# A second seven-product block in every up-projection group, and one fewer in every down-projection half

## The chip, the cores and the metric

The kernel runs on one core of a Trainium2 chip. The metric is the device time of one execution in microseconds, as the median of several runs. A profiled execution gives a trace of the engines: TensorE (PE, with its weight loads as PEld), VectorE (DVE), ScalarE (ACT), GpSimd (POOL, which only issues transfers here) and SyncE (SP, which issues the weight loads from HBM).

## The reference, cut to what matters

The program is a two-layer encoder trunk on 256 rows of 2048 features. Each layer is a mixer (attention of several kinds) and then a gated feed-forward part; a final normalisation ends it. The change lies in the feed-forward parts, which are

```python
def conv_ffn(x, w_up, conv_w, conv_b, w_down):
    h = jnp.einsum("bsd,df->bsf", x, w_up)              # 2048 -> 2 * 5632
    g, u = h[..., :D_FF], h[..., D_FF:]
    gp = jnp.pad(g, ((0, 0), (1, 1), (0, 0)))
    g = conv_w[0] * gp[:, :-2] + conv_w[1] * gp[:, 1:-1] + conv_w[2] * gp[:, 2:] + conv_b
    return jnp.einsum("bsf,fd->bsd", jax.nn.gelu(g) * u, w_down)   # 5632 -> 2048
```

and before each of them `rmsnorm` of the rows. All data are float32.

## The kernel before, in words

**A product in three.** A float32 number is split into a high part (rounded by a cast on ACT, `split`, L231) and a low part (what the cast left, a subtraction on DVE, L234). A float32 product becomes three products on PE: high by high, high by low, low by high (L195 to L197). A weight *unit* is a tile of 128 by 1024, that is two blocks of 128 features by 512 columns; `wunit` loads it (`raw`, five buffers), splits it (`wh` and `wl`, four buffers each), and `a_products` issues 12 matmuls for it: two blocks, two halves of the rows, three products.

**Seven products for eight.** Two units of two neighbouring column chunks, with 256 features and 256 rows, form a 2 by 2 by 2 block product, which needs eight block products or, by the known scheme of Winograd, seven. `column_forms` makes the sums of the weights (four DVE subtractions of 128x512, L951 to L955) and splits them; `form_sums` makes the sums of the activations, with `split` after it; `seven_products` issues 21 matmuls (L977 to L979) where two units issue 24. Three of the seven results go straight into the accumulators (`gm`), four go into banks of their own (`extra`: tags `s` and `tp`) and are added on DVE later.

**The feed-forward part.** `ffn` runs two halves (`HALVES`: six and five groups). `up_group(layer, j)` makes 512 columns of the gate (side x = 0) and of the other branch (x = 1) from 16 units: u = 0 to 3 of both sides by turns, then the rest of side 0, then the rest of side 1. At u = 3 (`UPK`) both sides' units are one seven-product block; its extra results are summed by `extra_parts` (L844 to L848) and scaled by `scaled_parts` (L856). At the end of a side, DVE scales and adds the two accumulators into a tile (L878; `sc` for side 0, `z` for side 1) and transposes it in 32 by 32 pieces (`turned`, L279); 16 transfers then move the pieces into place (`moved`, L273: 12 issued by POOL, 4 by SP). When side 0 has landed, `convolved` does the convolution in the next group (ACT L896, then two DVE instructions for each of four feature tiles, L897 and L899, then GELU, L901). When side 1 has landed, `multiplied` multiplies (L928) and splits the result into the activations of the down projection (`prod`). For the groups j - g0 in the third entry of `HALVES`, it also makes the activation sums of a seven-product block (`row_forms`).

**The down projection.** After a half's groups, `chunk_pair` does column chunks 0 and 1, then 2 and 3: its head (`pair_head`) takes both chunks by turns and does the blocks in `seven` as seven products; the rest follows chunk by chunk.

**Order.** The code's `later` and `tick` say after which unit a deferred step is written. A scheduler then sets the order in which each engine's instructions stand. On the chip each engine takes its instructions in that order, and a waiting instruction holds up those behind it.

Of the kernel before, what the change touches and what calls it, by code (L numbers as in the profile page):

```python
# [27 lines left out]
F32 = mybir.dt.float32  # L28
F32R = mybir.dt.float32r
AF = mybir.ActivationFunctionType  # L30
# [3 lines left out]
P = 128  # L34
# [13 lines left out]
RAW = 5  # L48
AHEAD = 4
LAST = 2  # L50
UPK = 3
HALVES = ((0, 6, (1, 2, 3)), (6, 11, (1, 2, 3)))


def rev2(ap):
# [16 lines left out]
def trunk_kernel(ctx: ExitStack, tc, a, out):  # L72
    nc = tc.nc
    V, S, G, T = nc.vector, nc.scalar, nc.gpsimd, nc.tensor

    const = ctx.enter_context(tc.tile_pool(name="const", bufs=1))
    wts = ctx.enter_context(tc.tile_pool(name="wts", bufs=4))
    acts = ctx.enter_context(tc.tile_pool(name="acts", bufs=1))
    att = ctx.enter_context(tc.tile_pool(name="att", bufs=2))
    tmp = ctx.enter_context(tc.tile_pool(name="tmp", bufs=2))  # L80
# [5 lines left out]
    def nm(s):  # L86
        uid[0] += 1
        return f"{s}_{uid[0]}"
# [5 lines left out]
    def later(delay, fn, rank=2):  # L94

        pending.append((now[0] + delay, rank, fn))
# [19 lines left out]
    def tps(tag, bufs):  # L116
        return psum.tile([P, 512], F32, name=nm(tag), tag=tag, bufs=bufs)
# [187 lines left out]
    def turned_rows(c, gain, res):  # L305

        z = att.tile([P, 2, 512], F32, name=nm("z"), tag="sc", bufs=1)
        V.transpose(z, h[:, :, c * 512:(c + 1) * 512])
        pf = att.tile([P, 8, P], F32, name=nm("hT"), tag="pt", bufs=2)
        moved(z.rearrange("p t k -> p (t k)"), pf)  # L310

        def tiles():
            for j in range(4):
                res[c * 4 + j] = y_tile(pf.rearrange("p (t j) q -> p j t q", t=2)[:, j], gain, c * 4 + j)
            if res is formed.get("of") and c == UPK // 2:
                y_forms(pf.rearrange("p (t j) q -> p j t q", t=2), gain)
        return tiles

    formed = {}

    def form_sums(a11, a21, a12, a22):

        f = tmp.tile([P, 4, P], F32, name=nm("sums"), tag="scc")
        V.tensor_tensor(f[:, 0], a21, a22, op=ALU.add)
        V.tensor_tensor(f[:, 1], f[:, 0], a11, op=ALU.subtract)
        V.tensor_tensor(f[:, 2], a11, a21, op=ALU.subtract)
        V.tensor_tensor(f[:, 3], a12, f[:, 1], op=ALU.subtract)
        return f

    def y_forms(src, gain):  # L330

        y = tmp.tile([P, 2, 2, P], F32, name=nm("yf"), tag="ry")
        for k in range(2):
            S.activation(y[:, k], src[:, UPK % 2 * 2 + k], AF.Copy, scale=gain[:, 2 * UPK + k:2 * UPK + k + 1])
        f = form_sums(*(y[:, k, t] for k in range(2) for t in range(2)))
        form = []
        for x, tag in enumerate(("R", "Rq")):
            high = tmp.tile([P, 2, P], F32R, name=nm("form"), tag="t0")
            low = const.tile([P, 2, P], F32R, name=nm("form"), tag=tag, bufs=1)
            split(high, low, f[:, 2 * x:2 * x + 2])  # L340
            form += [(high[:, k], low[:, k]) for k in range(2)]
        formed["form"] = form

    def row_factor(pin=False, late=False):

# [209 lines left out]
    yT = []  # L555
# [276 lines left out]
    yT = mixer_out(a["ev_out"], mix, ln[:, 2, :])  # L832


    def up_group(layer, j, yT, rstd, prod, *more):

        sides, extra, sums = {}, [], []
        src = [a["up"][layer, j, x] for x in range(2)]

        def extra_parts():  # L840

            b1, b5, b6, b7 = extra
            s1, x0, x1, y1 = (tmp.tile([P, 512], F32, name=nm("sum"), tag=tag) for tag in ("rx", "ry", "ry", "rx"))
            S.copy(s1, b1)  # L844
            V.tensor_tensor(x0, s1, b6, op=ALU.add)  # L845
            V.tensor_tensor(x1, x0, b7, op=ALU.add)
            V.tensor_tensor(x0, x0, b5, op=ALU.add)
            V.tensor_tensor(y1, x1, b5, op=ALU.add)  # L848
            sums.extend([[s1, x1], [x0, y1]])
            later(1, scaled_parts)  # L850

        def scaled_parts():

            for x in range(2):
                for t in range(2):
                    S.activation(sums[x][t], sums[x][t], AF.Copy, scale=rstd[0][:, t:t + 1])  # L856

        pss = [[tps("gm", 4), tps("gm", 4)] for _ in range(2)]
        for u in range(4):
            if not j and u == 2:  # L860
                rstd.append(row_factor())
            if u == UPK:
                extra += [tps("s", 2), tps("tp", 2), tps("tp", 2), tps("s", 2)]
                seven_products(pss, extra, column_forms(src, u, True), u, yT, formed["form"], True, True)
                later(1, extra_parts)
            else:
                for x in range(2):
                    a_unit(pss[x], src[x], u, yT, KT)
            tick()
        for x in range(2):  # L870
            for u in range(4, 8):
                a_unit(pss[x], src[x], u, yT, KT)
                if u % 2 == 1:
                    tick()
            z = (tmp.tile([P, 8, P], F32, name=nm("z"), tag="z", bufs=1) if x else
                 new_sc().rearrange("p t (f k) -> p (t f) k", k=P))
            for t in range(2):
                out = V.scalar_tensor_tensor(z.rearrange("p (f t) k -> p t f k", t=2)[:, t],  # L878
                                       pss[x][t].rearrange("p (f k) -> p f k", k=P), rstd[0][:, t:t + 1],
                                       sums[x][t].rearrange("p (f k) -> p f k", k=P), op0=ALU.mult, op1=ALU.add)  # L880
                if t:
                    tc.keep_in_program_order(out)
            sides[x] = quad(2 * x)
            turned(z.rearrange("p b k -> p (b k)"), sides[x].rearrange("p f (t k) -> p (f t) k", k=P), (3,))
            if not x:
                later(2, lambda: convolved(layer, j, sides))
        later(2, lambda: multiplied(j, sides, prod, *more))
# [14 lines left out]

    def new_forms(g0, n):

        if n == 0:
            high = tmp.tile([P, 4, P], F32R, name=nm("form"), tag="rw", bufs=1)
            return [(high[:, 2 * x:2 * x + 2], att.tile([P, 2, P], F32R, name=nm("form"), tag="bias", bufs=2))
                    for x in range(2)]
        if g0:
            t = acts.tile([P, 2, 4, P], F32R, name=nm("form"), tag=f"act{18 + 2 * n}")  # L910
        else:
            t = att.tile([P, 2, 4, P], F32R, name=nm("form"), tag="pt", bufs=2)
        return [(t[:, 0], t[:, 1])]

    def row_forms(c4, parts):

        f = form_sums(*(c4[:, 2 + k, t * P:(t + 1) * P] for k in range(2) for t in range(2)))
        form = []
        for high, low in parts:
            n = high.shape[1]  # L920
            split(high, low, f[:, len(form):len(form) + n])
            form += [(high[:, x], low[:, x]) for x in range(n)]
        return form
# [42 lines left out]
    def seven_products(pss, extra, w, u, act, form, first, last):  # L966

        def block(k, t):
            return [act[2 * u + k][:, x, t * P:(t + 1) * P] for x in range(2)]

        s1, s2, s3, s4 = form
        b1, b5, b6, b7 = extra
        for ps, (ah, al), (wh, wl) in zip(
                (pss[0][0], pss[1][0], b1, b7, b5, b6, pss[0][1]),
                (block(1, 0), s4, block(0, 0), s3, s1, s2, block(1, 1)), w):
            own = any(ps is x for x in extra)
            T.matmul(ps, ah, wh, start=own and first, stop=False)  # L977
            T.matmul(ps, ah, wl, start=False, stop=False)  # L978
            T.matmul(ps, al, wh, start=False, stop=own and last)  # L979
# [51 lines left out]
    def ffn(layer, yT, gain, last=False):  # L1031
        rstd, res = [], None
        for g0, g1, seven in HALVES:
            prod, forms = [], {}
# [13 lines left out]
    yT = ffn(0, yT, ln[:, 1, :])  # L1048
# [109 lines left out]
    for hh in range(2):  # L1158
        vt = v_tiles(gemm_a(a["od_v"][hh], yT, KT), rstd, ((18, 19, 20, 21), (16, 17, 22, 23))[hh])
        for hd in range(hh * 4, hh * 4 + 4):  # L1160
            y = att.tile([P, 6, 64], F32, name=nm("nb"), tag="bias", bufs=2)
# [8 lines left out]
            q, k = qk_tiles([a["od_qk"][hd * 2 + x] for x in range(2)], yT, (Rq, R), (rev, None), hd % 2 * 2)  # L1170
            later(2, lambda hd=hd, q=q, k=k, vt=vt, y=y: d_head(hd, q, k, vt, y))
    yT = mixer_out(a["od_out"], mix, ln[:, 3, :])
# [156 lines left out]
def _paired_up(w):  # L1329

    w = w.copy()
    x, y = w[:, :, 0, UPK].copy(), w[:, :, 1, UPK].copy()
    w[:, :, 0, UPK] = np.concatenate([x[..., :512], y[..., :512]], axis=-1)
    w[:, :, 1, UPK] = np.concatenate([y[..., 512:], x[..., 512:]], axis=-1)
    return w


# [69 lines left out]
```

## Time and profile before

| what | value |
|---|---|
| median of 3 runs | 2412.46 us (2407.63 to 2412.59) |
| the profiled execution's own time | 2409.76 us |
| its span | 2407.9 us |
| PE busy, weight loads busy | 99%, 82% of the span |
| DVE, ACT, POOL busy | 77%, 57%, 22% |
| mean granted TensorE clock | 0.999 |
| DMA traffic | 505.64 MB, mean 210 GB/s |

The span is what the profile covers from the first to the last instruction; the execution's own time is 1.9 us more. A matmul's row shows its time through the array, so that matmuls that follow each other overlap in the trace; busy shares of PE therefore tell whether PE was ever empty, not how fast it went. Rows of the timeline give the start in us, the length, the engine, line and operation, the tiles (out<-in), how many instructions are merged, and in brackets how long the engine had been idle and what ended that.

### The profile page before, as it was taken

How to read it: one execution, taken by the hardware profiler on the slowest of the kernel's cores; microseconds unless marked ns; L12 is line 12 of the kernel's file. 1: busy time of each engine (PE TensorE's matmuls, PEld its weight loads, DVE VectorE, ACT ScalarE, POOL GpSimd, SP SyncE). 2: the span in 40 equal slices, each digit the busy share in tenths (PEclk: the TensorE clock that was granted, in tenths of full speed). 3: DMA queues.
4: the chain of work that ended last, by engine and by line, in shares of the span. 5: the costliest groups of instructions: out<-in, count | busy, mean ns of one | idle time of the engine just before them, and what ended most of it. 6: DMA issues, size and time to landing. Idle time of an engine off the chain costs nothing.

```text
span 2407.9 us, 32958 instructions
## 1 busy us (share of the span) xinstructions
PE 2387.8 (99%) x10895; PEld 1982.4 (82%) x10895; DVE 1860.2 (77%) x2461; ACT 1374.0 (57%) x1954; POOL 538.8 (22%) x940
## 2 busy tenths in 40 slices
PE   9999999999999999999999999999999999999998
PEld 7888888888888888888788888888888888888787
DVE  6576567666778888778889868676788887788887
ACT  7455455566656565445656657555565654456564
POOL 1132033322222422004232100422223320033220
PEclk9999999999999999999999999999999999999999
DMA  8778678766777877668777764667778876687874
GB/s 309 203 195 239 196 196 239 216 201 184 218 200 221 213 214 217 202 206 219 213 217 211 221 201 138 193 197 211 201 214 225 208 227 195 207 219 209 236 212 156
DMA packets 287531, 505.64 MB, mean 210 GB/s; under 512 B 159096, under 2 KB 160504, under 8 KB 287360
## 3 DMA queue, kind: packets, MB, share of 16 engines
q1 hardware_dynamic: 256848, 470.15, 65.0%
q0 software_dynamic: 30080, 32.74, 8.0%
q8 instruction: 85, 1.39, 0.2%
q14 instruction: 86, 0.70, 0.1%
q10 hardware_dynamic: 432, 0.66, 0.1%
HBM read 458.48 MB, written 2.18 MB: 191 GB/s over the span
## 4 chain that ended last, share of the span: by engine, by line
PE 45%; DVE 3%; DMA 1%; issue 1%; ACT 1%; SPq 0%; POOL 0%; DVEq 0%; ACTq 0%
PE gm L197 12%; PE gm L196 12%; PE gm L195 12%; PE gm L145 2%; PE gm L150 1%; DVE wl L234 1%; PE gm L978 1%; PE gm L979 1%; PE gm L977 1%; PE tp L978 1%; DVE form L234 1%; DMA qk<-z 1%; ACT wh L231 1%; PE tp L979 0%; PE s L979 0%
## 5 line engine op out<-in xcount | busy, mean ns | idle before, releaser
L231 ACT CAST wh<-raw 128x1024 fp32r<-128x1024 f32 (+1 forms) x897 | 935.7, 1048 | 820.7 <-PE gm L197 651.5
L234 DVE TENSOR_TENSOR wl<-raw,wh 128x1024 fp32r<-128x1024 f32 (+1 forms) x897 | 1085.1, 1216 | 391.3 <-ACT wh L231 384.1
L195 PE MATMUL gm<-wh,yT 128*128 128x512 f32 x2092 | 816.1, 390 | 0.0
L196 PE MATMUL gm<-wl,yT 128*128 128x512 f32 x2092 | 814.7, 389 | 0.3 <-DVE wl L234 0.3
L197 PE MATMUL gm<-wh,yT 128*128 128x512 f32 x2092 | 814.6, 389 | 0.0
L197 PEld LDWEIGHTS gm<-wh,yT 128*128 128x128 f32 x2092 | 392.6, 188 | 82.2 <-DVE yT L240 0.2
L196 PEld LDWEIGHTS gm<-wl,yT 128*128 128x128 f32 x2092 | 392.8, 188 | 81.8 <-DVE wl L234 1.4
L195 PEld LDWEIGHTS gm<-wh,yT 128*128 128x128 f32 x2092 | 392.8, 188 | 80.9 <-ACT junk L265 0.4
L273 POOL DMA_DIRECT2D qk<-sc x264 | 151.7, 583 | 863.9 <-issue 389.6
L273 POOL DMA_DIRECT2D qk<-z x392 | 225.6, 584 | 257.7 <-DVE z L279 227.2
L195 PE MATMUL gm<-wh,prod 128*128 128x512 f32 x518 | 201.5, 389 | 0.0
L197 PE MATMUL gm<-wh,prod 128*128 128x512 f32 x518 | 201.5, 389 | 0.0
L196 PE MATMUL gm<-wl,prod 128*128 128x512 f32 x518 | 201.5, 389 | 0.0
L195 PEld LDWEIGHTS gm<-wh,prod 128*128 128x128 f32 x518 | 97.2, 188 | 20.3
L196 PEld LDWEIGHTS gm<-wl,prod 128*128 128x128 f32 x518 | 97.2, 188 | 20.2
L197 PEld LDWEIGHTS gm<-wh,prod 128*128 128x128 f32 x518 | 97.2, 188 | 20.2
L196 PE MATMUL gm<-wl,mix 128*128 128x512 f32 x256 | 100.1, 391 | 0.9 <-DVE wl L234 0.9
L195 PE MATMUL gm<-wh,mix 128*128 128x512 f32 x256 | 100.0, 391 | 0.0
L197 PE MATMUL gm<-wh,mix 128*128 128x512 f32 x256 | 99.6, 390 | 0.0
L273 POOL DMA_DIRECT2D hT<-z x72 | 41.4, 583 | 199.8 <-PE gm L197 75.5
L856 ACT ACTIVATE sum<-sum,rstd 128x512 f32<-128x512 f32 x88 | 59.7, 718 | 17.7 <-DVE sum L845 10.0
L145 PE MATMUL gm<-yT,wh 128*128 128x512 f32 x256 | 59.5, 390 | 0.0
(356 smaller groups left out, 2644.1 us busy)
## 6 DMA issues: line engine op xcount, KB each, us to landing
raw<-in_up SPq DMA_DIRECT2D x352, 512.0 KB, 4.5
raw<-in_down SPq DMA_DIRECT2D x176, 512.0 KB, 4.4
raw<-in_eva_qk SPq DMA_DIRECT2D x96, 512.0 KB, 4.3
raw<-in_eva_v SPq DMA_DIRECT2D x46, 512.0 KB, 6.0
raw<-in_evb_qk SPq DMA_DIRECT2D x32, 512.0 KB, 4.7
raw<-in_ev_out SPq DMA_DIRECT2D x32, 512.0 KB, 4.3
raw<-in_od_qk SPq DMA_DIRECT2D x32, 512.0 KB, 4.3
raw<-in_od_out SPq DMA_DIRECT2D x32, 512.0 KB, 4.3
```

The lines of the kernel that those rows point to most:

```text
L145: T.matmul(ps.rearrange("p a b -> p (a b)"), wh[:, k * P:(k + 1) * P], act[u * 8 + k].rearrange("p a b -> p (a b)"), start=(u == 0 and k = ...
L150: T.matmul(ps[:, 1, :], wl[:, k * P:(k + 1) * P], act[u * 8 + k][:, 0, :], start=False, stop=(u * 8 + k == KT - 1))
L195: T.matmul(ps[t], ah, wh[:, sl], start=(kt == 0), stop=False)
L196: T.matmul(ps[t], ah, wl[:, sl], start=False, stop=False)
L197: T.matmul(ps[t], al, wh[:, sl], start=False, stop=(kt == nk - 1))
L231: first = S.copy(dst_h, src)
L234: V.tensor_tensor(dst_l, src, dst_h.bitcast(F32), op=ALU.subtract)
L273: (nc.sync if i in on_sync else G).dma_start(dst[j * 32:(j + 1) * 32, :, i * 32:(i + 1) * 32], z[i * 32:(i + 1) * 32].rearrange("p (b j c) ...
L856: S.activation(sums[x][t], sums[x][t], AF.Copy, scale=rstd[0][:, t:t + 1])
L977: T.matmul(ps, ah, wh, start=own and first, stop=False)
L978: T.matmul(ps, ah, wl, start=False, stop=False)
L979: T.matmul(ps, al, wh, start=False, stop=own and last)
```

## The change

Each up-projection group has seven-product blocks at u = 3 and u = 5 (`UPKS`), so that units 0 to 5 of both sides go by turns and only units 6 and 7 are done side by side; the four extra banks collect both blocks and are summed after the second. Each half of the down projection has two blocks (j - g0 = 1, 2) instead of three. The activation sums for u = 5 are made once per layer (`y_forms`) and live in the buffers `rw` and `bias`, which the third down block used.

```diff
-UPK = 3
-HALVES = ((0, 6, (1, 2, 3)), (6, 11, (1, 2, 3)))
+UPKS = (3, 5)
+HALVES = ((0, 6, (1, 2)), (6, 11, (1, 2)))
...
-            if res is formed.get("of") and c == UPK // 2:
-                y_forms(pf.rearrange("p (t j) q -> p j t q", t=2), gain)
+            for n, u in enumerate(UPKS):
+                if res is formed.get("of") and c == u // 2:
+                    y_forms(pf.rearrange("p (t j) q -> p j t q", t=2), gain, n, u)
...
         pss = [[tps("gm", 4), tps("gm", 4)] for _ in range(2)]
-        for u in range(4):
+        heads = UPKS[-1] + 1
+        for u in range(heads):
             if not j and u == 2:
                 rstd.append(row_factor())
-            if u == UPK:
-                extra += [tps("s", 2), tps("tp", 2), tps("tp", 2), tps("s", 2)]
-                seven_products(pss, extra, column_forms(src, u, True), u, yT, formed["form"], True, True)
-                later(1, extra_parts)
+            if u in UPKS:
+                if not extra:
+                    extra += [tps("s", 2), tps("tp", 2), tps("tp", 2), tps("s", 2)]
+                seven_products(pss, extra, column_forms(src, u, True), u, yT, formed[u], u == UPKS[0], u == UPKS[-1])
+                if u == UPKS[-1]:
+                    later(1, extra_parts)
             else:
                 for x in range(2):
                     a_unit(pss[x], src[x], u, yT, KT)
             tick()
         for x in range(2):
-            for u in range(4, 8):
+            for u in range(heads, 8):
                 a_unit(pss[x], src[x], u, yT, KT)
```

The host's layout of the weights follows (`_paired_up`). In the rows below, a name's number tells one tile from the next; a line behind L315 is 6 to 10 higher in the changed kernel than before.

Where the instructions stand now, first on DVE at the end of an up group (the fifth of the first half, layer 0). `wl` is the low part of one weight unit. Before, from the end of side 0 to the end of side 1:

```order
L878 SCALAR_TENSOR_TENSOR sc_7935<-gm_7667,rstd_6182,sum_7850 128x4x128
L878 SCALAR_TENSOR_TENSOR sc_7935<-gm_7668,rstd_6182,sum_7852 128x4x128
L279 STREAM_TRANSPOSE sc_7935<-sc_7935 128x1024
L234 TENSOR_TENSOR wl_8013<-raw_8010,wh_8012 128x1024
L234 TENSOR_TENSOR wl_8070<-raw_8067,wh_8069 128x1024
L234 TENSOR_TENSOR wl_8088<-raw_8085,wh_8087 128x1024
L234 TENSOR_TENSOR wl_8106<-raw_8103,wh_8105 128x1024
L878 SCALAR_TENSOR_TENSOR z_8042<-gm_7669,rstd_6182,sum_7851 128x4x128
L878 SCALAR_TENSOR_TENSOR z_8042<-gm_7670,rstd_6182,sum_7853 128x4x128
L279 STREAM_TRANSPOSE z_8042<-z_8042 128x1024
```

Now, the same place:

```order
L888 SCALAR_TENSOR_TENSOR sc_8024<-gm_7704,rstd_6197,sum_7975 128x4x128
L234 TENSOR_TENSOR wl_8066<-raw_8063,wh_8065 128x1024
L888 SCALAR_TENSOR_TENSOR sc_8024<-gm_7705,rstd_6197,sum_7977 128x4x128
L234 TENSOR_TENSOR wl_8109<-raw_8106,wh_8108 128x1024
L279 STREAM_TRANSPOSE sc_8024<-sc_8024 128x1024
L888 SCALAR_TENSOR_TENSOR z_8081<-gm_7706,rstd_6197,sum_7976 128x4x128
L234 TENSOR_TENSOR wl_8127<-raw_8124,wh_8126 128x1024
L888 SCALAR_TENSOR_TENSOR z_8081<-gm_7707,rstd_6197,sum_7978 128x4x128
L234 TENSOR_TENSOR wl_8159<-raw_8156,wh_8158 128x1024
L279 STREAM_TRANSPOSE z_8081<-z_8081 128x1024
```

The transpose of side 0 stood four unit splits ahead of the first instruction of side 1; it now stands directly ahead of it (`wl_8066` belongs to the group's last unit, `wl_8109` to the next group's first).

On DVE in the next group, from the convolution on, before (`t` and `form` are the weight difference and its low part; the five raw-to-`wl` rows are two units and the three splits of the block):

```order
L899 SCALAR_TENSOR_TENSOR qk_8028<-qk_7938,convw,qk_8028 128x255 x2
L234 TENSOR_TENSOR wl_8173<-raw_8170,wh_8172 128x1024
L952 TENSOR_TENSOR raw_8192<-raw_8193,raw_8192 128x512
L234 TENSOR_TENSOR wl_8200<-raw_8193,wh_8199 128x1024
L234 TENSOR_TENSOR form_8210<-t_1509_8196,form_8209 128x512
L954 TENSOR_TENSOR raw_8193<-raw_8193,t_1509_8196 128x512
L234 TENSOR_TENSOR wl_8206<-raw_8192,wh_8205 128x1024
L955 TENSOR_TENSOR raw_8193<-raw_8193 128x512
L928 TENSOR_TENSOR qk_8028<-qk_8028,qk_8045 128x1024
L234 TENSOR_TENSOR wl_8214<-raw_8193,wh_8213 128x1024
```

Now:

```order
L909 SCALAR_TENSOR_TENSOR qk_8142<-qk_8027,convw,qk_8142 128x255 x2
L234 TENSOR_TENSOR wl_8253<-raw_8246,wh_8252 128x1024
L234 TENSOR_TENSOR wl_8259<-raw_8245,wh_8258 128x1024
L960 TENSOR_TENSOR raw_8246<-raw_8246,t_1535_8249 128x512
L957 TENSOR_TENSOR t_1552_8331<-raw_8327 128x512
L961 TENSOR_TENSOR raw_8246<-raw_8246 128x512
L234 TENSOR_TENSOR wl_8267<-raw_8246,wh_8266 128x1024
L934 TENSOR_TENSOR qk_8142<-qk_8142,qk_8084 128x1024
L234 TENSOR_TENSOR wl_8294<-raw_8291,wh_8293 128x1024
```

The splits of the first block all stand behind the convolution now, and the block's last split (`wl_8267`) follows directly on the subtraction that it needs (L961), where the multiplication stood between them before.

On SP at the same boundary, before:

```order
L273 DMA qk_7938<-sc_7935 32x8x32 x4
L128 DMA raw_8152<-in_up 128x1024
L128 DMA raw_8170<-in_up 128x1024
L939 DMA raw_8192<-in_up 128x1024
L940 DMA raw_8193<-in_up 128x1024
L273 DMA qk_8045<-z_8042 32x8x32 x4
```

Now:

```order
L128 DMA raw_8223<-in_up 128x1024
L273 DMA qk_8027<-sc_8024 32x8x32 x4
L945 DMA raw_8245<-in_up 128x1024
L273 DMA qk_8084<-z_8081 32x8x32 x4
L946 DMA raw_8246<-in_up 128x1024
L128 DMA raw_8291<-in_up 128x1024
```

The two loads of the first block stood ahead of SP's four moves of side 1; the second of them now stands behind those.

More of the change, by code (lines that the diff above doesn't have):

```diff
@@ L314, in tiles, with form_sums @@
                 res[c * 4 + j] = y_tile(pf.rearrange("p (t j) q -> p j t q", t=2)[:, j], gain, c * 4 + j)
-            if res is formed.get("of") and c == UPK // 2:
-                y_forms(pf.rearrange("p (t j) q -> p j t q", t=2), gain)
+            for n, u in enumerate(UPKS):
+                if res is formed.get("of") and c == u // 2:
+                    y_forms(pf.rearrange("p (t j) q -> p j t q", t=2), gain, n, u)
         return tiles
     formed = {}
-    def form_sums(a11, a21, a12, a22):
-        f = tmp.tile([P, 4, P], F32, name=nm("sums"), tag="scc")
+    def form_sums(tag, a11, a21, a12, a22):
+        f = tmp.tile([P, 4, P], F32, name=nm("sums"), tag=tag)
         V.tensor_tensor(f[:, 0], a21, a22, op=ALU.add)
@@ L328, in form_sums, with y_forms @@
         return f
-    def y_forms(src, gain):
+    def y_forms(src, gain, n, u):
         y = tmp.tile([P, 2, 2, P], F32, name=nm("yf"), tag="ry")
         for k in range(2):
-            S.activation(y[:, k], src[:, UPK % 2 * 2 + k], AF.Copy, scale=gain[:, 2 * UPK + k:2 * UPK + k + 1])
-        f = form_sums(*(y[:, k, t] for k in range(2) for t in range(2)))
+            S.activation(y[:, k], src[:, u % 2 * 2 + k], AF.Copy, scale=gain[:, 2 * u + k:2 * u + k + 1])
+        f = form_sums("scc", *(y[:, k, t] for k in range(2) for t in range(2)))
+        if n:
+            both = tmp.tile([P, 4, P], F32R, name=nm("form"), tag="rw", bufs=1)
         form = []
         for x, tag in enumerate(("R", "Rq")):
-            high = tmp.tile([P, 2, P], F32R, name=nm("form"), tag="t0")
-            low = const.tile([P, 2, P], F32R, name=nm("form"), tag=tag, bufs=1)
+            if n:
+                high = both[:, 2 * x:2 * x + 2]
+                low = att.tile([P, 2, P], F32R, name=nm("form"), tag="bias", bufs=2)
+            else:
+                high = tmp.tile([P, 2, P], F32R, name=nm("form"), tag="t0")
+                low = const.tile([P, 2, P], F32R, name=nm("form"), tag=tag, bufs=1)
             split(high, low, f[:, 2 * x:2 * x + 2])
             form += [(high[:, k], low[:, k]) for k in range(2)]
-        formed["form"] = form
+        formed[u] = form
     def row_factor(pin=False, late=False):
@@ L903, in new_forms @@
     def new_forms(g0, n):
[L905 to L908, printed above, removed]
         if g0:
-            t = acts.tile([P, 2, 4, P], F32R, name=nm("form"), tag=f"act{18 + 2 * n}")
+            t = acts.tile([P, 2, 4, P], F32R, name=nm("form"), tag=f"act{20 + 2 * n}")
         else:
@@ L915, in row_forms @@
     def row_forms(c4, parts):
-        f = form_sums(*(c4[:, 2 + k, t * P:(t + 1) * P] for k in range(2) for t in range(2)))
+        f = form_sums("ry", *(c4[:, 2 + k, t * P:(t + 1) * P] for k in range(2) for t in range(2)))
         form = []
@@ L1331, in _paired_up @@
     w = w.copy()
-    x, y = w[:, :, 0, UPK].copy(), w[:, :, 1, UPK].copy()
-    w[:, :, 0, UPK] = np.concatenate([x[..., :512], y[..., :512]], axis=-1)
-    w[:, :, 1, UPK] = np.concatenate([y[..., 512:], x[..., 512:]], axis=-1)
+    for u in UPKS:
+        x, y = w[:, :, 0, u].copy(), w[:, :, 1, u].copy()
+        w[:, :, 0, u] = np.concatenate([x[..., :512], y[..., :512]], axis=-1)
+        w[:, :, 1, u] = np.concatenate([y[..., 512:], x[..., 512:]], axis=-1)
     return w
```

## The prediction

> **What bounds the kernel now.** First the page: the span and the busy shares.
>
> ```profile
> span 2407.9 us, 32958 instructions
> PE 2387.8 (99%) x10895; PEld 1982.4 (82%) x10895; DVE 1860.2 (77%) x2461; ACT 1374.0 (57%) x1954; POOL 538.8 (22%) x940
> ```
>
> PE is almost never empty. Its rate is read from the table of stretches, one up group each, from one seven-product block to the next:
>
> ```profile
> core 0: us, PE busy (x) PEld busy (x) DVE busy (x) ACT busy (x) POOL busy (x), PEclk, DMA share, GB/s
> 720.65:763.55 42.90, 42.90 (x190) 35.48 (x189) 35.33 (x45) 24.56 (x31) 13.82 (x24) 1.00 0.80 219
> 763.55:807.79 44.24, 43.19 (x191) 35.39 (x189) 37.99 (x53) 25.95 (x35) 13.78 (x24) 1.00 0.81 219
> 807.79:851.93 44.14, 43.20 (x190) 35.40 (x189) 37.79 (x51) 26.13 (x35) 13.81 (x24) 1.00 0.78 213
> 895.90:938.80 42.90, 42.90 (x190) 35.48 (x189) 35.90 (x46) 25.25 (x33) 13.80 (x24) 1.00 0.80 220
> 1151.26:1195.21 43.95, 43.19 (x191) 35.40 (x190) 38.27 (x52) 26.31 (x37) 13.78 (x24) 1.00 0.78 218
> 1238.77:1282.51 43.74, 43.21 (x190) 35.40 (x189) 38.01 (x53) 26.55 (x36) 13.77 (x24) 1.00 0.80 221
> ```
>
> A group has 14 plain units of 12 matmuls and a block of 21, 189 in all. 42.90 us over 189 is 0.227 us for a matmul. Six of the 22 groups stand here: two without a stall, and four in which the activation sums of the group before (`row_forms`) fall. Those take 44.0 us on average, 1.1 us over. There are 12 such groups and 10 plain ones. Who waits there, in the table of waits:
>
> ```profile
> PE tp L978 <- DVE form L234: 8.0, 11, 1.2
> ACT qk L896 <- DMA qk<-sc: 11.1, 15, 1.5
> ```
>
> PE waits for DVE, at a seven-product block. In 15 of the 22 groups ACT stands before the convolution until side 0 (`sc`) has landed. So two chains run close beside PE: DVE's queue, and the way of side 0 over DMA. Both are seen at one group's end (PE finishes it at 879.55, 16.35 us or 72 matmuls ahead of the block at 895.90):
>
> ```profile
> 858.22 0.69 DVE L845 TENSOR_TENSOR sum<-sum,tp 128x512 f32<-128x512 f32 x1
> 858.82 1.23 DVE L234 TENSOR_TENSOR wl<-raw,wh 128x1024 fp32r<-128x1024 f32 x1
> 859.95 0.69 DVE L846 TENSOR_TENSOR sum<-sum,s 128x512 f32<-128x512 f32 x1
> ...
> 868.45 1.40 DVE L878 SCALAR_TENSOR_TENSOR sc<-gm,rstd,sum 128x512 f32<-128x512 f32 x2
> 869.89 1.25 DVE L279 STREAM_TRANSPOSE sc<-sc 128x1024 f32<-128x1024 f32 x1
> ...
> 879.29 1.40 DVE L878 SCALAR_TENSOR_TENSOR z<-gm,rstd,sum 128x512 f32<-128x512 f32 x2
> 880.73 1.25 DVE L279 STREAM_TRANSPOSE z<-z 128x1024 f32<-128x1024 f32 x1
> ...
> 885.76 0.87 DVE L897 SCALAR_TENSOR_TENSOR qk<-qk,convw,qk 128x255 f32<-128x255 f32 x2
> ...
> 888.91 1.22 DVE L234 TENSOR_TENSOR wl<-raw,wh 128x1024 fp32r<-128x1024 f32 x1
> ...
> 894.73 1.22 DVE L928 TENSOR_TENSOR qk<-qk,qk 128x1024 f32<-128x1024 f32 x1
> ...
> 897.13 1.43 DVE L234 TENSOR_TENSOR prod<-qk,prod 128x256 fp32r<-128x256 f32 x4
> 898.47 1.22 DVE L234 TENSOR_TENSOR wl<-raw,wh 128x1024 fp32r<-128x1024 f32 x1
> ```
>
> ```profile
> 884.50 2.08 ACT L896 ACTIVATE qk<-qk,convb,convw 128x256 f32<-128x256 f32 x4 [0.94 <-DMA qk<-sc]
> ```
>
> ```profile
> 871.71 6.88 POOL L273 DMA_DIRECT2D qk<-sc  x12 [26.19 <-issue]
> 882.26 4.60 POOL L273 DMA_DIRECT2D qk<-z  x8 [3.67 <-DVE z L279]
> 887.06 0.58 POOL L273 DMA_DIRECT2D qk<-z  x1 [0.19 <-issue]
> 887.92 1.73 POOL L273 DMA_DIRECT2D qk<-z  x3 [0.28 <-DMA qk<-z]
> ```
>
> Starts give what each instruction costs in DVE's queue: a unit split 1.13 (858.82 to 859.95), a 128x512 operation 0.60, the pair of scalings 1.44, a transpose 1.2, the convolution 3.15 (885.76 to 888.91), four activation splits 1.34; the multiplication is taken as a split. The transpose of side 0 ends at 871.14 and ACT starts at 884.50, 13.4 us later, of which POOL's issuing takes the first 7.5. The 15 waits average 0.74 against 0.94 here, so I take 13.1. That delay lies hidden now, because side 0 ends 10.9 us before side 1.
>
> **The change part by part.**
>
> *Matmuls.* 22 blocks are added in up groups; of down's 23 (the last pair of chunks had two of three) 16 are left. 15 blocks by 3 matmuls by 0.227 us is 10.2 us less for PE. By halves: an up group's PE time falls to 186 x 0.227 = 42.2; the 7 lost down blocks cost 7 x 3 x 0.227 = 4.8.
>
> *DVE and ACT work of a block.* A block adds four 128x512 operations and 1.5 unit splits on DVE: 2.4 + 1.7 = 4.1, and 1.5 casts on ACT, which has room at 25 of 43 us. DVE's busy time rises from 35.3 to 39.4 of 42.2, and to 42 where `row_forms` falls. So DVE would just do, if it never waited.
>
> *A wait inside a block.* The block's last split now follows directly on the subtraction it needs, with ACT's cast between. Rows of a down block where that is so already:
>
> ```profile
> 957.11 0.69 DVE L955 TENSOR_TENSOR raw<-raw 128x512 f32<-128x512 f32 x1
> 958.99 1.23 DVE L234 TENSOR_TENSOR wl<-raw,wh 128x1024 fp32r<-128x1024 f32 x1 [1.19 <-ACT wh L231]
> ```
>
> 1.88 us from start to start, so 1.28 beyond the 0.60 of the subtraction, twice per group. Before, the multiplication filled it.
>
> *Side 0 ends late.* This is the term that decides. Only two units of side 1 follow side 0, 5.5 us of PE where there were four and 10.9. And the order puts the transpose of `sc` right in front of side 1's scaling, behind the next group's first split. Landing then takes its 13.1 us, and behind the convolution, in order, stand on DVE all splits of the first block, the multiplication, the second block, the sums, and the next transpose of `sc`. That is a loop from one transpose to the next. Counted along the new order: landing 13.1; first ACT convolution 0.6; convolution 3.15; 13 unit splits 14.7 (three of the first block, u = 4 twice, three of the second, four in units 6 and 7, the next group's first); 11 operations of 128x512 6.6; multiplication 1.13; activation splits 1.34; scalings 1.44; transpose 1.2; two waits 2.56. The sum is 45.8 us for a group, against PE's 42.2. Where `row_forms` stands in it, four sums of 0.20 and a split of 0.60 are added (starts of the rows below): 47.2.
>
> ```profile
> 852.60 0.28 DVE L324 TENSOR_TENSOR sums<-qk 128x128 f32<-128x128 f32 x1
> 852.80 0.28 DVE L326 TENSOR_TENSOR sums<-qk 128x128 f32<-128x128 f32 x1
> ...
> 855.88 0.69 DVE L234 TENSOR_TENSOR form<-sums,form 128x512 fp32r<-128x512 f32 x1
> 856.48 1.23 DVE L234 TENSOR_TENSOR wl<-raw,wh 128x1024 fp32r<-128x1024 f32 x1
> ```
>
> PE waits out the difference at the splits behind the convolution. Each half's first group has no convolution in it: 42.2. In its second, one split stands ahead of the convolution and other work fills one wait partly: about 43.9. Of the remaining 14, 8 have `row_forms` (two per half), 6 have not. After: 4 x 42.2 + 4 x 43.9 + 8 x 47.2 + 6 x 45.8 = 996.8. Before: 10 x 42.9 + 12 x 44.0 = 957.0. Up groups: +39.8 us.
>
> *The head behind each half.* The last group's convolution falls into the down head. It starts 12.6 us after the last group's end (transpose 1.1 ahead of it, landing 13.1, ACT 0.6). Behind it stand 10 unit splits, 7 operations of 0.60, 3.15, 1.13, 1.34 and a wait of 1.28: 22.4, so the second block's last split is done at 35.0. PE could use it at 30.4 (16.35 + 4.8 + 5.45 + 3.8) but has up to 24 matmuls of the next units to fill in. Bounds 0 and 4.6; I take 2.5 in the middle, by four halves: +10.
>
> *Activation sums for u = 5.* 0.8 and two splits on DVE, two scalings and two casts on ACT, once per layer in the last chunk of the mixer's output projection, where no seven-product block competes. Taken as 0; without that cover at most 2 us a layer.
>
> *Extra banks held longer; buffers moved.* No other tile of the feed-forward part asks for these banks; 0.
>
> Sum: 39.8 + 10 + 4.8 = +54.6, on the span 2407.9: 2462.5; the execution is 1.9 longer than its span: 2464. The runs' median stands 2.7 above the profiled execution, so against the median I give 2467.
>
> **What is not shown: landing under the new spacing.** The two sets of moves now follow within 5 us. Rows that bound their price:
>
> ```profile
> qk<-sc POOLq DMA_DIRECT2D x264, 32.0 KB, 5.4
> hT<-z POOLq DMA_DIRECT2D x72, 32.0 KB, 2.2
> ```
>
> By the lower row, a move issued last (7.5 us) would land 2.2 later, at 9.7, and the loop would be 42.4: at PE's rate. I take 13.1, since its row is this very transfer among the same weight loads.
>
> [...]
>
> **The rivals.**
>
> *Side 0 still lands in time, faster.* The loop then falls below PE's 42.2, and DVE's sum decides: 39.4 + 2.6 for the waits = 42.0, with `row_forms` 43.4. Groups: 8 x 43.4 + 14 x 42.2 = 938.0 against 957.0, -19.0 + 4.8 = -14.2: 2398. It needs a landing of at most 9.5 us. For it: PE busy 99%. Against it: 13.4 in the row, and ACT already waiting in 15 of 22 groups. The point of no change is where 54.6 us over 18 convolutions and 4 heads vanish: 2.5 us, a landing of 10.6.
>
> [...]
>
> *The second set is late too.* POOL's rows for `z` show waits after eight moves, the last for a landing of the same set: at most about eight seem to be under way. With `sc` directly ahead, `z`'s issuing would stretch, and landing near 21 us after the group's end; the multiplication's turn is at about 22. If each landing takes 1 or 2 us more, the multiplication waits and every group pays about 2 us: 18 x 2 = +36, 2502. SP's order adds to it: the first block's second load now waits for the transpose of `z` and lands about 11 (median to landing 4.5 us below), close before the convolution at 12.6.
>
> ```profile
> raw<-in_up SPq DMA_DIRECT2D x352, 512.0 KB, 4.5
> ```
>
> *Little change.* Landing near 10.6, or waits that overlap better than counted: 2405 to 2435.
>
> **How the numbers follow.** Loop as counted, 2440 to 2485: 0.58. Second set late too, 2485 to 2510: 0.22. Little change to a small loss: 0.08. Side 0 in time: 0.12. Below 0.2% (5 us) a measurement here cannot tell a change. Slower: 0.58 + 0.22 + half of 0.08 and a little, 0.84; same 0.05; faster 0.11. The range leaves out the fast case and the tails: 2432 to 2505.
>
> **What would show it.** In the changed trace: side 0's transposes 13 us ahead of ACT's convolution, with ACT's wait on `qk<-sc` grown to some 2 us or more a group; DVE idle ahead of the convolution; PE stalls at blocks in all groups from the third of a half on; periods near 45.8 and 47.2 us, first groups near 42.2. Wrong would be the prediction if periods stay near 42 to 43 (landing shorter), or if the multiplication's wait on `qk<-z` is the longer one.

## The result, and the profile after

The changed kernel takes 2489.69 us (median of 4 runs, 2487.49 to 2493.9), the kernel before 2412.53 beside it: a ratio of 1.0326, 95% interval [1.0309, 1.0342]. It is slower by 77 us. The prediction was 2467 with a range of 2432 to 2505. The profiled execution, the longest of the four, took 2493.9 us, and its span is 84.2 us longer than before. Its page:

```profile
span 2492.1 us, 33069 instructions
PE 2417.1 (97%) x10850; PEld 1972.1 (79%) x10850; DVE 1916.0 (77%) x2539; ACT 1390.7 (56%) x1984; POOL 541.4 (22%) x940
```

45 matmuls are gone, as counted. DVE has 56 us more work, yet the same share of a longer span: no engine became full, and PE fell from 99% to 97%. Stretches by stage, from one first block to the next (columns as in the prediction): the first group of a half, the second, one with `row_forms`, and a plain one.

```profile
676.97:719.24 42.27, 42.27 (x188) 34.92 (x187) 36.09 (x44) 26.10 (x31) 13.85 (x24) 1.00 0.81 218
719.24:761.89 42.65, 42.54 (x187) 34.76 (x186) 35.82 (x46) 24.76 (x33) 12.66 (x22) 1.00 0.78 220
761.89:811.23 49.34, 44.63 (x187) 34.11 (x186) 41.32 (x57) 26.96 (x36) 13.94 (x26) 1.00 0.71 190
863.72:912.11 48.39, 45.84 (x186) 36.28 (x186) 40.12 (x52) 26.45 (x35) 12.68 (x23) 0.93 0.77 193
```

The group that has no convolution in it runs at PE's own 42.27. From the third on, the stretches of all halves take 46.8 to 52.5 us, 49 on average. Who waits (engine, line waited for, us in total, times, longest):

```profile
ACT wh L231 <- DVE raw L961: 98.4, 35, 3.2
DVE raw L958 <- DMA raw<-in_up: 34.4, 21, 3.1
ACT qk L906 <- DMA qk<-z: 30.0, 7, 6.3
PE gm L984 <- DVE wl L234: 18.0, 13, 1.6
PE gm L196 <- DVE wl L234: 15.2, 26, 1.5
PE tp L983 <- ACT wh L231: 14.3, 20, 0.9
```

PE now waits for splits (`wl`, `wh`) at the blocks and just behind them. ACT's cast waits for the last subtraction of a block (L961). ACT's convolution (L906) waits for the transfers; the row names `z`, but in the round below ACT goes on 0.07 us after the last piece of `sc` has landed, so the wait there is for side 0. All this is one chain, and one round of it can be read on DVE, from the end of side 0 to the next (a plain group):

```profile
841.81 1.23 DVE L279 STREAM_TRANSPOSE sc<-sc 128x1024 f32<-128x1024 f32 x1
...
846.72 1.24 DVE L279 STREAM_TRANSPOSE z<-z 128x1024 f32<-128x1024 f32 x1
...
854.39 0.69 DVE L957 TENSOR_TENSOR t<-raw 128x512 f32<-128x512 f32 x1 [4.19 <-DMA raw<-in_up]
...
861.30 0.98 DVE L907 SCALAR_TENSOR_TENSOR qk<-qk,convw,qk 128x255 f32<-128x255 f32 x2 [3.39 <-DMA qk<-z]
...
864.56 2.35 DVE L234 TENSOR_TENSOR wl<-raw,wh 128x1024 fp32r<-128x1024 f32 x2
...
868.03 0.69 DVE L961 TENSOR_TENSOR raw<-raw 128x512 f32<-128x512 f32 x1
869.89 1.23 DVE L234 TENSOR_TENSOR wl<-raw,wh 128x1024 fp32r<-128x1024 f32 x1 [1.17 <-ACT wh L231]
871.03 1.22 DVE L934 TENSOR_TENSOR qk<-qk,qk 128x1024 f32<-128x1024 f32 x1
...
881.73 1.23 DVE L234 TENSOR_TENSOR wl<-raw,wh 128x1024 fp32r<-128x1024 f32 x1 [1.19 <-ACT wh L231]
...
892.55 1.24 DVE L279 STREAM_TRANSPOSE sc<-sc 128x1024 f32<-128x1024 f32 x1
```

The transpose ends at 843.04, the convolution on DVE starts at 861.30, and DVE is idle for 8 of these 18 us. Then it works without a pause, but for two waits of 1.2 (and one of 0.2) for a cast, until the next transpose of side 0. ACT and POOL in the same round:

```profile
860.66 2.07 ACT L906 ACTIVATE qk<-qk,convb,convw 128x256 f32<-128x256 f32 x4 [4.92 <-DMA qk<-z]
```

```profile
843.62 4.61 POOL L273 DMA_DIRECT2D qk<-sc  x8 [30.86 <-DVE sc L279]
851.73 2.31 POOL L273 DMA_DIRECT2D qk<-sc  x4 [3.50 <-issue]
854.03 2.31 POOL L273 DMA_DIRECT2D qk<-z  x4
```

POOL issues eight moves of side 0, stands for 3.5 us and issues the last four: this landing took 17.5 us from the transpose, the longest of all.

For each kernel I cut every such round (transpose of `sc` to transpose of `sc`, as DVE's rows give it) at the convolution's first and last instruction. The means, in us, of the 14 rounds of a run that are neither a half's first nor its second group's:

| kernel | from the transpose to the convolution | convolution | behind it (DVE idle in that) | round |
|---|---|---|---|---|
| before | 14.28 | 3.17 | 26.33 (2.28) | 43.78 |
| after | 15.14 | 3.23 | 30.37 (2.93) | 48.74 |

Before, the round was about as long as a group on PE (42.9 without a stall), with some slack in it. After, it is 48.74, and PE needs 42.27.

### The profile page after: what moved, and what is told of

Same layout as the page of the kernel before. It is cut to its first block, busy times and chain, and to the rows that moved or that the text cites. A ratio compares the mean times of both kernels' runs of the same rounds, so it can differ in the third digit from the quotient of the medians.

```text
span 2492.1 us, 33069 instructions
## 1 busy us (share of the span) xinstructions
PE 2417.1 (97%) x10850; PEld 1972.1 (79%) x10850; DVE 1916.0 (77%) x2539; ACT 1390.7 (56%) x1984; POOL 541.4 (22%) x940
## 4 chain that ended last, share of the span: by engine, by line
PE 66%; DVE 14%; DMA 11%; issue 4%; ACT 2%; SPq 2%; POOL 1%; DVEq 0%; ACTq 0%; POOLq 0%
PE gm L196 17%; PE gm L197 17%; PE gm L195 17%; DVE wl L234 6%; DMA raw<-in_up 5%; DMA qk<-z 3%; PE gm L145 2%; ACT wh L231 2%; SPq L273 2%; DVE qk L907 1%; DVE qk L909 1%; DMA raw<-in_down 1%; DMA qk<-sc 1%; PE gm L150 1%; PE gm L984 1%
## 5 line engine op out<-in xcount | busy, mean ns | idle before, releaser
L234 DVE TENSOR_TENSOR wl<-raw,wh 128x1024 fp32r<-128x1024 f32 (+1 forms) x912 | 1098.9, 1215 | 338.8 <-ACT wh L231 330.2
L196 PE MATMUL gm<-wl,yT 128*128 128x512 f32 x1916 | 748.9, 391 | 12.7 <-DVE wl L234 12.7
L195 PE MATMUL gm<-wh,yT 128*128 128x512 f32 x1916 | 744.4, 392 | 3.8 <-ACT wh L231 3.8
L197 PE MATMUL gm<-wh,yT 128*128 128x512 f32 x1916 | 746.4, 390 | 0.0
L196 PEld LDWEIGHTS gm<-wl,yT 128*128 128x128 f32 x1916 | 359.8, 188 | 96.9 <-DVE wl L234 23.7
L195 PEld LDWEIGHTS gm<-wh,yT 128*128 128x128 f32 x1916 | 359.7, 188 | 85.5 <-ACT wh L231 11.7
L197 PEld LDWEIGHTS gm<-wh,yT 128*128 128x128 f32 x1916 | 359.7, 188 | 74.3 <-DVE yT L240 0.2
L196 PE MATMUL gm<-wl,prod 128*128 128x512 f32 x574 | 223.8, 390 | 1.6 <-DVE wl L234 1.6
L197 PE MATMUL gm<-wh,prod 128*128 128x512 f32 x574 | 223.4, 389 | 0.0
L195 PE MATMUL gm<-wh,prod 128*128 128x512 f32 x574 | 221.8, 390 | 0.9 <-ACT wh L231 0.9
L195 PEld LDWEIGHTS gm<-wh,prod 128*128 128x128 f32 x574 | 107.8, 188 | 24.8 <-ACT wh L231 2.6
L197 PEld LDWEIGHTS gm<-wh,prod 128*128 128x128 f32 x574 | 107.7, 188 | 22.2
L906 ACT ACTIVATE qk<-qk,convb,convw 128x256 f32<-128x256 f32 x88 | 45.8, 591 | 71.5 <-DMA qk<-z 30.0
L958 DVE TENSOR_TENSOR raw<-raw,raw 128x512 f32<-128x512 f32 x60 | 41.3, 689 | 48.1 <-DMA raw<-in_up 34.4
```

What stands on the lines that cost most here:

```text
L195: T.matmul(ps[t], ah, wh[:, sl], start=(kt == 0), stop=False)
L196: T.matmul(ps[t], ah, wl[:, sl], start=False, stop=False)
L197: T.matmul(ps[t], al, wh[:, sl], start=False, stop=(kt == nk - 1))
L234: V.tensor_tensor(dst_l, src, dst_h.bitcast(F32), op=ALU.subtract)
L906: S.activation(c, g, AF.Identity, scale=convw[:, layer, 1, f:f + 1], bias=convb[:, layer, f:f + 1])
L958: V.tensor_tensor(w12, w22, w12, op=ALU.subtract)
```

## The experiments

All are variants of the changed kernel. The kernel before took 2410 to 2412 us beside them.

**The down part alone.** `UPKS = (3,)` in place of `(3, 5)`; two blocks in a down half.

> One part alone: the up groups keep their single block at u = 3, the down halves have two blocks instead of three. Theory (the loop over side 0's landing): side 0 ends four units ahead as before, so nothing of the loss appears. PE has 7 blocks less, 7 x 3 x 0.227 = 4.8 us more; 8 instead of 12 groups carry activation sums, with 1.1 us of stall each, 4.4 us less. Sum about 0: 2413, range 2406 to 2419. Rival (the down halves lose more than counted, because the third block hid something): 2425 or more.

2404.36 us (2403.17 to 2406.68), ratio 0.9975 [0.9966, 0.9985]: it beats the kernel before. The lost down blocks cost 0.64 us each (a stretch with one fewer takes 63.96 for 63.32), but the stalls at up blocks fell from 11.9 us to 3.7, by more than the four groups that lost their `row_forms`. With only one kind of down sums left, they are also written and split differently (into other buffers); which of the two did it stays open. So the loss is all in the up part: 85.3 us above this version.

**Side 0 early, second block kept.**

```diff
-UPKS = (3, 5)
+UPKS = (1, 3)
```

> The same number of blocks and the same work on every engine as in the changed kernel, but the up groups' two blocks lie at u = 1 and u = 3 instead of 3 and 5, so that the last four units of each side are done side by side again and side 0 ends 10.9 us ahead of side 1. Theory (side 0 lands late): its transpose is again some 8.8 us ahead of side 1's scaling, it lands about 4 to 5 us into the next group, and the loss is gone: DVE's counted work (42.0 us a group, 43.4 with activation sums) or PE's 42.2 sets the period, 2395 to 2420. Rival (DVE is simply full with two blocks a group): no change to the changed kernel, 2470 to 2500.

2428.12 us (2426.42 to 2433.23), ratio 1.0077 [1.0059, 1.0094]: 61.6 us of the 77 come back, so DVE is not full with two blocks. 8 us above the theory's range remain. Side 0's transpose ends 8.9 us ahead of side 1's second scaling again (8.8 before, 1.9 in the changed kernel), but the round is 44.39 (13.42, 3.26 and 27.71): the loop is shorter, and still longer than 42.2. Directly behind the convolution PE waits for the first of three splits (DVE's row, then PE's):

```profile
757.31 3.49 DVE L234 TENSOR_TENSOR wl<-raw,wh 128x1024 fp32r<-128x1024 f32 x3
```

```profile
758.59 0.51 PE L984 MATMUL tp<-wl,form 128*128 128x512 f32 x1 [0.86 <-DVE wl L234]
```

**Side 0 late, without a second block.** Two blocks per down half, and one per up group, at u = 5:

```diff
-UPKS = (3, 5)
+UPKS = (5,)
```

> One block per up group, at u = 5 instead of u = 3 (so side 0 ends as late as in the changed kernel, but DVE and ACT have no second block), two blocks per down half. Theory (the time from one transpose of side 0 to the next is a sum, landing plus DVE's work behind the convolution): one block less takes 4.1 of DVE's work and 1.3 of waiting out of it, 45.8 to 40.4, and 41.8 with activation sums, both under PE's 42.9, so nearly nothing is lost against the version with the block at 3 (2404): 2403 to 2420. Rival (a late side 0 costs by itself, whatever DVE has to do): 2450 to 2475.

2448.13 us (2438.59 to 2451.78), ratio 1.0141 [1.0121, 1.0162]: the rival's number. A late side 0 costs about 44 us without any second block (the four runs spread over 13 us). The round is 45.73 (16.09, 3.27 and 26.39), longer than PE's 42.9, but my 40.4 for it was wrong. I started from the forecast's 45.8 where a plain round had measured 48.4, and took the whole block out of it, 5.4 us, of which half a split and two subtractions had stood ahead of the convolution, under the landing, where they cost nothing. Landing was also longer here, 15.3 us for 14.1. DVE now has less to do ahead of the convolution, and waits:

```profile
847.25 1.22 DVE L234 TENSOR_TENSOR wl<-raw,wh 128x1024 fp32r<-128x1024 f32 x1 [1.50 <-DMA qk<-z]
853.61 0.97 DVE L907 SCALAR_TENSOR_TENSOR qk<-qk,convw,qk 128x255 f32<-128x255 f32 x2 [5.14 <-ACT qk L906]
...
869.43 4.63 DVE L234 TENSOR_TENSOR wl<-raw,wh 128x1024 fp32r<-128x1024 f32 x4 [1.19 <-ACT wh L231]
```

Behind the convolution one split, two subtractions and one wait have gone (25.58 in a plain group for 29.23).

**No landing.**

```diff
             if not x:
+                sides[3] = z.rearrange("p (f t) k -> p f (t k)", t=2)
...
-        g4, c4 = sides[0], quad(4)
+        g4, c4 = sides[3], quad(4)
```

> The changed kernel, where the convolution reads side 0's transposed tile from before the moves (the rows and features are then permuted; that part of the computation is left out). All moves are still made, all work on every engine stays; only the wait for side 0's landing is gone. Theory (side 0's landing): the period falls to DVE's own sum or PE's, with some stall left where the multiplication waits for side 1 or the first block for its second load: 2400 to 2435. Rival (DVE full): 2470 to 2500.

2434.9 us (2431.1 to 2439.67), ratio 1.0102 [1.0083, 1.0121]: 54.8 us come back, just inside the theory's range. The convolution now starts 2.5 us behind the transpose, and what stood under the landing stands behind it: a round is 44.6 us (2.5, 5.5 and 36.6, with 4.0 of waits), still more than PE's 42.2. What PE waits for now is the last splits of the blocks:

```profile
PE tp L985 <- DVE wl L234: 17.8, 25, 1.5
PE s L985 <- DVE wl L234: 7.3, 8, 1.2
```

**The wait inside a block.** The last unit's two halves are split one after the other, so that the first does not wait for the second's subtraction. (`ring` gives a `wh` and a `wl` tile, `apart` splits a whole tile and names its halves.)

```diff
         V.tensor_tensor(w22, w22, t1, op=ALU.subtract)
-        V.tensor_tensor(w21, w21, w22, op=ALU.subtract)
-        p11, p3 = apart(ring(), ra)
         if odd:
+            p11, p3 = apart(ring(), ra)
+            y = ring()
+            p2, p4 = ([x[:, k * 512:(k + 1) * 512] for x in y] for k in range(2))
+            split(*p2, w22)
+            V.tensor_tensor(w21, w21, w22, op=ALU.subtract)
             p1, = ...
-            p2, p4 = apart(ring(), rb)
+            split(*p4, w21)
```

In the changed kernel:

> The changed kernel (blocks at u = 3 and 5) with each block's last unit split in two halves of 512 columns. Theory (the wait for the cast is a term of the loop, 1.28 us twice in each of 18 loops and once in each head): shorter by 20 to 36 us, 2455 to 2470. Rival (the wait lies beside the landing of side 0 and costs nothing): 2485 to 2495.

2431.26 us (2420.33 to 2445.99), ratio 1.0093 [1.006, 1.0126]: 58 us less, far more than expected; the profiled execution was one of its shortest (span 2418.6).

```profile
853.67 0.68 DVE L966 TENSOR_TENSOR raw<-raw 128x512 f32<-128x512 f32 x1
854.28 1.82 DVE L234 TENSOR_TENSOR wl<-raw,wh 128x512 fp32r<-128x512 f32 x2
856.01 1.22 DVE L934 TENSOR_TENSOR qk<-qk,qk 128x1024 f32<-128x1024 f32 x1
```

The waits are gone: DVE's idle time behind the convolution fell from 2.93 to 0.22 a round. That is the 2.56 that the prediction counted and a little more, 38 us in 14 rounds. (My own 20 to 36 for this run was less than two waits in 18 rounds make, 46.) Most of the rest came ahead of the convolution, 15.14 to 13.86; why the landing was shorter too is not settled.

With blocks at 1 and 3 the same edit does nothing good:

> Blocks at u = 1 and 3 (side 0 ends early again), and each block's last unit is split in two halves of 512 columns, so that the first half's split starts one subtraction earlier and the second half's cast runs beside other DVE work. Theory (what is left of the loss with blocks at u = 1 and 3 is the wait for the cast inside a block, about 1.3 us twice a group): about 20 us less than 2428, 2405 to 2420. Rival (these waits are hidden, and what is left is the convolution standing ahead of the splits in DVE's order): 2425 to 2432.

2437.34 us (2434.6 to 2442.35), ratio 1.0116 [1.0103, 1.013], 9 us more than without it, outside both expectations. The round grew from 44.39 to 45.00, behind the convolution (28.31 for 27.71). There the order took in one subtraction and gave half a split to the part ahead, which is no more work, but DVE waits 1.84 us for 1.42; why the halves did not end these waits here is open.

And with one block per group, as a candidate:

> One block per up group at u = 3 and two per down half, as in the version with the down part of the change alone (2404.4), with each block's last unit split in two halves. Theory (one block per group leaves DVE no loop longer than PE's time, and the wait is covered by the multiplication): the same as that version within 0.3%, 2398 to 2410. Rival (part of the 1 us that groups with activation sums lose is that wait): 2390 to 2398.

2404.65 us (2402.55 to 2407.0), ratio 0.9976 [0.9967, 0.9985], the same as without halves (2404.36): PE's stalls at up blocks are only 3.7 us in all there, and the wait is hidden.

**The landing, by who issues it.** Side 0's 16 moves are issued 12 by POOL and 4 by SP. First 8 and 8:

```diff
-            turned(..., (3,))
+            turned(..., (3,) if x else (1, 3))
```

> The changed kernel, with 8 of side 0's 16 moves issued by SP instead of 4, so that GpSimd issues 8 (4.6 us) instead of 12 (6.9 us). Theory: landing after the transpose falls from 13.6 by up to 2.3 us, and the period of each group with a convolution falls by as much where landing ends the wait; the first block's second load, which SP issues later by 0.5 to 1 us, limits that to 1 or 2 us a group: 2455 to 2480. Rival (DVE full): no change, within 5 us of 2490. Rival (the loads behind SP's moves decide): slower than 2490, by 10 us or more.

2475.22 us (2470.83 to 2477.01), ratio 1.0263 [1.0244, 1.0281], 14 us less. Landing fell from 13.4 us (mean of all 22) to 8.2, more than the issuing saves; POOL, with only eight moves of the set, no longer stands in the midst of it (they take 4.60 us in the round below). But the round fell by 1.6 only. SP's eight moves of side 0 and four of side 1 now stand ahead of the block's loads, and nearly the whole first block stands behind the convolution (34.1, with 4.35 idle):

```profile
796.74 5.71 SPq L273 DMA_DIRECT2D qk<-sc  x8
802.80 2.56 SPq L273 DMA_DIRECT2D qk<-z  x4
805.47 0.54 SPq L945 DMA_DIRECT2D raw<-in_up  x1
```

```profile
811.33 0.69 DVE L957 TENSOR_TENSOR t<-raw 128x512 f32<-128x512 f32 x1 [1.87 <-DMA raw<-in_up]
```

Then all 16 by POOL:

```diff
-            turned(..., (3,))
+            turned(..., (3,) if x else ())
```

> The changed kernel with all 16 moves of side 0 issued by POOL instead of 12 by POOL and 4 by SP. Theory (landing of side 0 is a term of the loop, and POOL's issuing and its limit of about eight moves under way set it): landing grows by 2.3 us or more, in 18 loops and 4 heads about 25 to 45 us, 2515 to 2535. Rival (the loop is bound by DVE's own work, not by the landing): 2485 to 2495. SP's weight loads are queued behind nothing of side 0 then, which could give back up to 1 us a loop: 2500.

2468.38 us (2465.89 to 2472.57), ratio 1.0245 [1.0231, 1.0259]: faster by 21 us, against both. Landing did grow, to 17.5 us. But SP's loads come earlier (the first block's first subtraction starts at 850.62 in the round below, for 854.39 in the changed kernel's), and the scheduler put the whole first block under the landing, so that two splits, three subtractions and nearly all waits fewer stand behind the convolution. The block's last split, and then the convolution:

```profile
857.02 1.22 DVE L234 TENSOR_TENSOR wl<-raw,wh 128x1024 fp32r<-128x1024 f32 x1
862.51 0.69 DVE L957 TENSOR_TENSOR t<-raw 128x512 f32<-128x512 f32 x1 [4.28 <-DMA raw<-in_up]
863.12 0.88 DVE L907 SCALAR_TENSOR_TENSOR qk<-qk,convw,qk 128x255 f32<-128x255 f32 x2
```

The round is 19.48, 3.36 and 23.48 (0.10 idle), 46.32: 4.3 more ahead, 6.9 less behind. The sum holds; what I had not thought of is that the edit changes both terms.

8 and 8 with blocks at 1 and 3, without and with halves:

> Blocks at u = 1 and 3, two per down half, and side 0's 16 moves issued 8 by SP and 8 by POOL instead of 4 and 12. Theory (the time from one transpose of side 0 to the next is landing plus DVE's work behind the convolution; with blocks at 1 and 3 it is 43 to 45 us against PE's 42.2): the landing falls from 12.9 to about 8.2 us, and the loop by as much as DVE waits ahead of the convolution, 2 us, so 2428 becomes 2395 to 2410. Rival (SP's loads of the blocks come later behind eight moves, and DVE waits for them instead): 2425 to 2460.

> The same with each block's last unit split in two halves of 512 columns. Theory (the landing and the waits inside the blocks are both terms of the loop, and both are shortened): 2390 to 2410. Rival (waits for the loads take their place): 2425 to 2460.

2471.0 us (2466.65 to 2474.98), ratio 1.0256 [1.0238, 1.0275], and 2490.22 (2483.08 to 2495.75), ratio 1.0332 [1.0309, 1.0355]. Both are slower than blocks at 1 and 3 alone (2428), as the rival said, though beyond its range. Landing fell from 12.9 to 7.5 us. But the convolution moved forward in DVE's order, ahead of `z`'s transpose and the end of the first block, and what stands behind it rose from 27.71 to 33.87 and 35.73, with 3.79 and 5.54 of waits in it. In the second of them:

```profile
760.53 0.69 DVE L958 TENSOR_TENSOR raw<-raw,raw 128x512 f32<-128x512 f32 x1 [1.70 <-DMA raw<-in_up]
...
781.98 1.23 DVE L234 TENSOR_TENSOR wl<-raw,wh 128x1024 fp32r<-128x1024 f32 x1 [2.15 <-ACT wh L231]
```

**Two blocks only where they ran at PE's rate.** In the first three groups of a half two blocks, else one; halves; two per down half.

```diff
+TWO = (0, 1, 2)
-        heads = UPKS[-1] + 1
+        ups = UPKS if j - more[1] in TWO else UPKS[:1]
+        heads = ups[-1] + 1
...
```

`more[1]` is the half's first group.

> Two blocks (u = 3 and 5) in the first three groups of each half, one block (u = 3) in the others, halves of the last unit, two blocks per down half. With two blocks and halves the first three periods of a half were at 42.3 to 42.8 (PE's own time), the later ones at 43 to 47. Theory (the loop is short where no activation sums and no second late side meet): 12 groups by 0.64 to 0.68 us less than the version with one block and halves (2404.6): 2395 to 2399. Rival (the groups behind a late side 0 pay 1 to 2 us each): 2404 to 2420.

2414.29 us (2411.57 to 2419.37), ratio 1.0014 [1.0005, 1.0023]: inside the rival's range. The first two periods of each half stood at 42.3, but the third and fourth at 43.9 to 46.4: both carry `row_forms` and start behind a late side 0, the fourth with one block only. No version with a second block in an up group beat one block; the best are the two at 2404.4 and 2404.6.

## Why the prediction was right in kind, and 23 us short

*The loop was the cause, as predicted.* First groups 42.27 (forecast 42.2), second ones 43.69 (43.9), then 48.44 plain (45.8) and 48.96 with `row_forms` (47.2). No engine is full, and the two edits that each took one term out, the landing and the cast waits, gave back 55 and 58 of 77 us. A late side 0 alone costs about 44 us; a second block with side 0 early costs 24; both together cost 85, all against one block at u = 3. The 18 beyond the sum fits the second block's work standing behind a late landing; no run shows it by itself.

*The mis-sized terms.* By steps of the loop, means of the 14 rounds: landing, taken as 13.1 from the row before, was 14.08 (11.6 to 17.5); the start of the convolution after it, taken as ACT's 0.6, was 1.06; the convolution 3.23 for 3.15; and the rest, 28.95 and 30.35 as counted, was 29.53 and 31.00. That is 2.1 us a round, 30 us in 14, and accounts for the 28 us by which up groups exceed the forecast (about +68 for +39.8). Against the medians the forecast is only 23 us short, because the profiled execution took 4 us more than the runs' median, where the one before took 3 less. The largest single miss is "I take 13.1, since its row is this very transfer among the same weight loads": the row was, but POOL's longer standing (its issuing of a set ended 8.6 us after the transpose on average, for 7.8 before) was not in it, nor `z`'s set right behind; what share the latter has is not shown. The rival "The second set is late too" had named both, and was right that landing would cost 1 us more; it was wrong that the multiplication would pay. Before the multiplication DVE waited 0.9 us in all 22 groups together, since the convolution ahead of it on DVE had moved as far.

*Heads.* The stalls in the four down heads sum to about 13 us for 10, inside the bounds of 0 and 18.

*Down blocks.* 0.64 us a block, so +4.5 for +4.8. Not foreseen: with one block per group, the stalls at up blocks fall by 8 us when one set of `row_forms` per half goes. Whether that holds in the changed kernel, where the loop is longer than a group on PE, no run shows.

*The cast waits* were 2.56 together in plain groups, as counted, but with a little luck: the two took 2.36, and a third that was not counted took 0.2.

*A side sum* of the prediction is slightly off by its own terms: 36 us more than 2467 is 2503, not 2502. It does not touch the forecast.

*The lower bound on landing.* The lower row that the prediction set beside its own, a move landed 2.2 us after its issue, gave a loop of 42.4 us. In the changed kernel and the one before, the medians of POOL's moves of `sc` are 5.2 and 5.4. With 8 and 8 and blocks at 1 and 3 the median is 2.2:

```profile
qk<-sc POOLq DMA_DIRECT2D x176, 32.0 KB, 2.2
```

Even there the round was 46.81, not the 42.4 that the prediction worked out from such a landing for the changed kernel's order, since more of DVE's work stood behind the convolution (33.87 us for 30.37). PE was the busiest engine before (99%, weight loads 82%, DVE 77%); it was relieved of 45 matmuls, and the time rose by 77 us.

## What to carry to other kernels

Find the loop: from one instruction to its next occurrence, through transfers and other engines, add up what stands in order, and compare the sum with the busiest engine's time; an engine at 99% can hide a loop that is about as long as its own period, and saving work on that engine then gains nothing. Count as a term only what is queued behind the late event, since work ahead of it lies under the wait and costs nothing. Where a scheduler sets the order, look at both parts after every edit: here a landing longer by 4 us gained 21 us, and one shorter by 5 us lost 43, by what the order put on either side of it.

## What the runs showed of the hardware

*PE at half rate behind two stalls close together.* At the plain group above PE waited about 3.1 us for the block's first matmul and 1.9 us, one matmul later, for its second. What came then:

```profile
863.72 0.73 PE L983 MATMUL gm<-wh,yT 128*128 128x512 f32 x1 [2.96 <-ACT wh L231]
865.83 0.80 PE L984 MATMUL gm<-wl,yT 128*128 128x512 f32 x1 [1.38 <-DVE wl L234]
...
868.13 0.63 PE L983 MATMUL s<-wh,yT 128*128 128x512 f32 x1
868.56 0.63 PE L984 MATMUL s<-wl,yT 128*128 128x512 f32 x1
868.98 0.63 PE L985 MATMUL s<-wh,yT 128*128 128x512 f32 x1
...
871.61 0.40 PE L983 MATMUL gm<-wh,yT 128*128 128x512 f32 x1
871.84 0.40 PE L195 MATMUL gm<-wh,yT 128*128 128x512 f32 x1
```

Ten matmuls start 0.427 us apart instead of 0.227; the granted clock stands at 0.50 for 6.8 us there, and at 0.93 over the whole stretch. Such a row of matmuls at half rate stands at four places among the up groups of this trace, 35 matmuls in all, 7 us: a small part of the loss. Each follows a stall of 1.9 us with another, of 0.8 to 3.1 us, one matmul ahead of it. One such pair (0.9 and 1.9 us) has none at half rate behind it, and neither have the six stalls of 1.6 to 1.9 us that stand alone. The other runs differ much in this: no up group of the runs without landing or with halves in the changed kernel has any (mean granted clock 1.000 and 0.999 over the profiled execution, 0.995 in the changed kernel's), and the slowest, with 8 and 8, blocks at 1 and 3 and halves, has 119 of them, 24 us of PE's time (0.985). How much of its time that cost no run shows.

The granted clock of this trace stands at 0.50 in four stretches among the up groups, from 863.83, 915.03, 1276.84 and 1939.03, for 6.83, 3.41, 6.83 and 3.41 us. The longest single stall ahead of them is 3.1 us, and two of the four places have stalls of only 2.7 us in all ahead of them, as much as the pair that has no matmul at half rate behind it. What sets the clock to 0.50 the runs do not show.

*POOL's moves.* In the changed kernel's order a set's landing took 17.5 us where POOL issues 16 of its moves, 13.4 with 12, 8.2 with 8 (means of 22). In ten of the changed kernel's 22 sets POOL stood for 0.6 us or more after eight moves; nine times it went on 0.3 us after the first of them had landed, and in the round above, where it stood longest, 1.6 us after. In the round shown with 16 it stood for 0.99 us after eleven, of which three had landed, and went on 0.3 us after the fourth. In the traces of the changed kernel and of the one before, with 925 transfers issued by POOL in each, never more than eight of them are under way at a time, counted from the start of the issue to the landing; the set of eight in the round shown with 8 and 8 was issued in 4.60 us, without such a stand.
